# First loads on three queues, the position bias table behind the evictions, and four PSUM banks for the first projection of a two-block transformer kernel

## The chip, the cores and the metric

One core of one Trainium2 chip runs the kernel. The metric is the device time of one execution in microseconds; the time of before is the median of three runs. Engines are named as in the profile: PE is TensorE (PEld its weight loads), DVE VectorE, ACT ScalarE, POOL GpSimd, SP SyncE; a q behind the name means the engine's queue of DMA issues.

## What is computed

Two transformer blocks in a row on 512 tokens of width 1024, in float32. The change touches the start of the first block alone:

```
xn = rmsnorm(x, attn_norm_g)
proj = xn @ w_in                       # 1024 x 2312
qa, ka, va, qb, kb, vb, f_logit = split(proj)
qa, ka = rmsnorm per head of 64        # 8 query heads, 2 key heads
out_a = sliding-window attention (window 128) with sinks and the
        position bias  -slope_h * (t - s),  slope_h = 2 ** -(h + 1)
log_f = log_sigmoid(f_logit + b_forget);  c = cumsum(log_f over tokens)
out_b = causal softmax attention of qb, kb, vb with the bias c[t] - c[s]
x = x + concat(out_a, out_b) @ w_out
x = x + relu(rmsnorm(x) @ w_up) ** 2 @ w_down
```

The second block (conditioning, neighbourhood attention, pooling, a second MLP) follows and isn't touched.

## The kernel before

Every matrix operand is split into a high and a low float32r part (`split`, L147 and L148: ScalarE copies the high part, VectorE subtracts it), and a product is three matmuls, high by high, high by low, low by high (`mm3`, L152 to L154).

`attention_one` begins with the loads. The four token tiles `xin` (128 tokens by 1024) come by `fetch_x` (L346), the gain vector `g_attn` (128 x 8) by L349. The projection goes in six blocks c of output columns. Block 0 has 392 columns (four query heads, a key head, a value head, the 8 forget logits), and its weights come in four parts kp of 256 rows each; a part is fetched in four pieces of 256, 64, 64 and 8 columns (`part_of`, which calls `fetch`, L169). Then come the small loads of `misc`: four norm gains of 64 values (L365), the sinks, the forget bias and a few constants (L370 to L372), then `alibi0` (L376), a 128 x 256 table of distances, and the causal mask. All of these are issued by SyncE's queue, in the order of the code.

`project(0)` turns each token tile on TensorE (`turned`, L216, written `n_0t` to `n_3t` in the rows), splits it into `xnT`, multiplies the weight part by the gain and splits it (L183 on ScalarE gives `w_0h` to `w_3h`, L184 on VectorE `w_0l` to `w_3l`), and accumulates eight row groups for each token tile in one PSUM bank (`pj`). `close(t)` evicts a tile on ScalarE into `pjs`, scaled by the token's 1/rms (L407), and `finish` takes it to the head norm, the value tiles and the turned heads (`ta`, L490; `qa` and `kah` on ScalarE, L464 to L471). `square` (L256) makes the sum of squares of a token tile. Tiles 0 and 1 are accumulated side by side as the weight parts come; tiles 2 and 3 follow. The ring "x" of PSUM banks for `pj` has two banks, 0 and 1, so tile 2 needs the bank of tile 0, and its product can't begin before tile 0's eviction. When tile 2 is done, the loads of block 1 (`load(1)`) are asked for; block 1's rows read `w_0` to `w_3` too, with 384 columns. Two raw buffers hold its parts, so its third part is fetched when the first is split.

After `project_a(0)` ScalarE makes the position bias table of all heads, `alibi`, in eight activations from `alibi0` (L742), which the scores of the windowed attention read (L605). Then `gates` (L540 to L566) takes the forget logits `zf` through exp and log (`az`, L541 and L542), a cumulative sum on TensorE by a triangular matrix (`cps`, L558, from `trir` and `lfh`), and the attention of pairs of heads runs interleaved with the projection of the next block.

```
self.banks(x=(0, 1), o=(2,), t=(3, 4, 7), s=(5, 6))
...
for _ in project_a(0):
    pass
tab = self.gp.tile([P, 8, 256], F32, tag="g", name="alibi")
for h in range(8):
    ac(out=tab[:, h, :], in_=alibi0, func=AF.Copy, scale=-(2.0 ** -(h + 1)))
```

The code is written in this order, but each engine's own order of instructions is decided when the kernel is built, by a planner that follows a model of durations, and the loads' order on a queue with it. Each engine then works through its instructions in order.

Of the kernel before, what the change touches and what calls it, by code (L numbers as in the profile page):

```python
# [8 lines left out]
F32 = mybir.dt.float32  # L9
F32R = mybir.dt.float32r  # L10
AF = mybir.ActivationFunctionType
# [5 lines left out]
P = 128  # L17
SEQ = 512
D = 1024
# [12 lines left out]
C_ALIBI = 0  # L32
# [75 lines left out]
RB = 1.5  # L108
PBUF = 3
RATIO = 1.6  # L110
TURN = "vavp"
TURNA = "vvvp"
TURNB = "vvva"
# [16 lines left out]
class Build:  # L130
# [32 lines left out]

        return self.parts(name, self.fetch(name, srcs, a, b), a, b, gain, eng)

    def fetch(self, name, srcs, a, b, rv=None):
        rv = (self.raw(name) if rv is None else rv)[:, 0:a * b].rearrange("p (a b) -> p a b", a=a)
        for o, src in srcs:
            self.nc.sync.dma_start(out=rv[:, :, o:o + src.shape[2]], in_=src)  # L169
        return rv  # L170

    def parts(self, name, rv, a, b, gain=None, eng=None, own=None):
# [130 lines left out]
    def attention_one(self, ph):  # L303
        tc, nc, a = self.tc, self.nc, self.a
        tp = ph.enter_context(tc.tile_pool(name="t1", bufs=2, reuse_waits="tile"))
        cst = a["consts"]
        ac = nc.scalar.activation
# [3 lines left out]
        def const(name, shape, dt=F32):  # L311
            return tp.tile(shape, dt, name=name, tag=name, bufs=1)

        def prob(which, name, shape, dt=F32R):
            return tp.tile(shape, dt, tag="pt" + which, name=name, bufs=3)

        g = const("g_attn", [P, KC])
# [4 lines left out]
        for i in range(4):  # L322
            segs.append([(768 + 128 * i, 128), (1280 + 128 * i, 128), (1792 + 128 * i, 128)])

        def part_of(c, kp, rv=None):

            srcs, o = [], 0
            for s, w in segs[c]:
                srcs.append((o, self.kview(a["w_in"], 2 * kp, 2, s, w)))
                o += w  # L330
            return self.fetch(f"w{c}_{kp}", srcs, 2, o, rv), (2, o, g[:, 2 * kp:2 * kp + 2])

        def load(c):
            tiles = []
            for kp in range(4):
                rv, (n, w, gain) = part_of(c, kp)
                tiles.append(self.parts(f"w{c}_{kp}", rv, n, w, gain, nc.gpsimd if c > C1 and kp in KPG else None))
                yield 0.0
            loaded[c] = tiles
# [5 lines left out]
        def fetch_x(t):  # L345
            nc.sync.dma_start(out=xin[t], in_=a["x"][0, t * P:(t + 1) * P, :])  # L346

        fetch_x(0)
        nc.sync.dma_start(out=g, in_=a["attn_norm_g"].rearrange("(k p) -> p k", p=P))  # L349
        first = []  # L350
        for kp in range(4):
            first.append(part_of(0, kp, None if kp < 2 else prob("hl"[kp % 2], f"w0r{kp}", [P, D], F32)))
            if kp == 1:
                fetch_x(1)
        fetch_x(2)
# [2 lines left out]
        r1 = const("r1", [P, NT])  # L358
# [4 lines left out]
        for nm, col in gn.items():  # L363
            src = a[nm]
# [7 lines left out]
        nc.sync.dma_start(out=misc[:, 24:38], in_=cst[:, C_COEF:C_COEF + 14])  # L372
        for nm in ("q_norm_a", "q_norm_b"):
            nc.gpsimd.tensor_scalar(out=gn[nm], in0=gn[nm], scalar1=0.125, scalar2=0.0, op0=ALU.mult, op1=ALU.add)
        alibi0 = const("alibi0", [P, 256])
        nc.sync.dma_start(out=alibi0, in_=cst[:, C_ALIBI:C_ALIBI + 256])  # L376
        causal = const("causal", [P, P], F32R)
        identr = const("identr", [P, P], F32R)
        ctmp = tp.tile([P, P], F32, tag="p", name="ctmp", bufs=3)
# [5 lines left out]
        def project(c, finish):  # L385

            n = sum(w for _, w in segs[c])
            if c and c not in loaded:
                yield from load(c)
            tiles = loaded.pop(c) if c else []  # L390
            accs = {}

            def part(t, kp):
                if kp == 0:
                    accs[t] = self.ps("x", f"pj{c}_{t}")
                cols = slice(t * P, (t + 1) * P)
                wh, wl = tiles[kp]
                for i in range(2):
                    k = 2 * kp + i
                    xq = xnT[k // 4]  # L400
                    self.mm3(accs[t][:, 0:n], xq[:, k % 4, 0, cols], xq[:, k % 4, 1, cols], wh[:, i, :], wl[:, i, :],
                             k == 0, k == KC - 1)
                    yield 0.48

            def close(t):
                s = tp.tile([P, 392], F32, tag="pj", name=f"pjs{c}_{t}", bufs=2)
                ac(out=s[:, 0:n], in_=accs[t][:, 0:n], func=AF.Copy, scale=r1[:, t:t + 1])  # L407
                finish(t, s)

            def square(t):  # L410
                self.inv_rms(xin[t], r1, t, f"r1_{t}", self.part("wl", f"xs{t}", F32))

            turns = range(NT)
            if c == 0:
                turns = (2, 3)
                for kp in range(4):
                    if kp < 2:
                        self.split_T(xin[kp], xnT, kp, f"n1_{kp}")
                    rv, (a_, w, gain) = first[kp]
                    tiles.append(self.parts(f"w0_{kp}", rv, a_, w, gain))  # L420
                    if kp == 0:
                        yield from part(0, 0)
                    else:
                        if kp == 1:
                            yield from part(0, 1)
                            yield from part(1, 0)
                            yield from part(1, 1)
                        else:
                            square(kp - 2)
                            yield from part(0, kp)  # L430
                            yield from part(1, kp)
                for t in (2, 3):
                    self.split_T(xin[t], xnT, t, f"n1_{t}")
                for t in range(2):
                    close(t)
                    square(t + 2)
            for t in turns:
                for kp in range(4):
                    yield from part(t, kp)
                close(t)  # L440
                if t == NT - 2 and c + 1 < len(segs):
                    yield from load(c + 1)

        def head_norm(s, nh, name):

            w = 64 * nh
            sq = tp.tile([P, 384], F32, tag="sq", name=name + "sq", bufs=1)
            nc.gpsimd.tensor_tensor(out=sq[:, 0:w], in0=s[:, 0:w], in1=s[:, 0:w], op=ALU.mult)
            ss = self.small("ss", name + "ss")
            nc.vector.tensor_reduce(out=ss[:, 0:nh], in_=sq[:, 0:w].rearrange("p (h d) -> p h d", h=nh), axis=AX.X, op=ALU.add)  # L450
            r = self.rstd(ss[:, 0:nh], nh, 64, name + "r")
            qn = tp.tile([P, 384], F32, tag="qn", name=name + "qn", bufs=2)
            nc.gpsimd.tensor_tensor(out=qn[:, 0:w].rearrange("p (h d) -> p h d", d=64),
                                    in0=s[:, 0:w].rearrange("p (h d) -> p h d", d=64),
                                    in1=r[:, 0:nh].unsqueeze(2).to_broadcast([P, nh, 64]), op=ALU.mult)
            return qn
# [4 lines left out]
        def put_q(dst, src, gain, h, cols):  # L461

            me, other = slice(64 * h, 64 * h + 64), slice(64 - 64 * h, 128 - 64 * h)
            ac(out=dst[me, cols], in_=src[me, :], func=AF.Copy, scale=gain[me, :])  # L464
            stt(out=dst[other, cols], in0=src[me, :], scalar=gain[me, :], in1=dst[me, cols].bitcast(F32), op0=ALU.mult, op1=ALU.subtract)
# [34 lines left out]
        def project_a(i):  # L500
            pa = Pairs(f"ta{i}")

            def finish(t, s):
                if i == 0:
                    nc.vector.tensor_tensor(out=zf[:, t, :], in0=s[:, 384:392], in1=bfor, op=ALU.add)
                qn = head_norm(s, 5, f"a{i}{t}")
                self.split(va[i][0][:, t, 0:64], va[i][1][:, t, 0:64], s[:, 320:384])
                pa.put(t, [qn[:, 0:P], qn[:, P:2 * P], qn[:, 2 * P:2 * P + 64]])
                if t % 2 == 1:
                    cols = slice((t - 1) * P, (t + 1) * P)  # L510
                    for h in range(4):
                        put_q(qa[4 * i + h], pa.get(h // 2), gn["q_norm_a"], h % 2, cols)
                    put_k(*ka[i], pa.get(2), gn["k_norm_a"], 0, cols, True)
            yield from project(i, finish)
# [147 lines left out]
        def attn_b(pair, q, k, v):  # L662
# [61 lines left out]
            for x in range(len(units) + LA + 1):  # L724
# [8 lines left out]
                if y >= 0 and y % 2 == 1:  # L733
                    u, h, _ = units[y]
                    values(u, h)
                    yield CB * 0.8

        for _ in project_a(0):
            pass
        tab = self.gp.tile([P, 8, 256], F32, tag="g", name="alibi")  # L740
        for h in range(8):
            ac(out=tab[:, h, :], in_=alibi0, func=AF.Copy, scale=-(2.0 ** -(h + 1)))  # L742
        mixT.append(self.quad("mixT0"))
        b = {}
        gates()
# [258 lines left out]
    def attention_two(self, ph, hxT):  # L1004
# [90 lines left out]
        def attn(i, qT, kT, kcT, v, tb):  # L1095
# [3 lines left out]
            def scores(u, h, nn):  # L1099
# [16 lines left out]
                nc.vector.reciprocal(out=den[:, 0:1], in_=den[:, 0:1])  # L1116
                self.scaled(pr, den[:, 0:1], TURN[(2 * u + h) % 2 * 2 + nn])

# [105 lines left out]
        for i in range(4):  # L1224
            interleave(attn(i, *r[i]), fill[i], RATIO)

# [224 lines left out]
```

## Time and profile before

| what | us |
|---|---|
| median of 3 runs | 1255.92 (1253.18 to 1258.51) |
| the profiled execution's own time | 1260.07 |
| its span, first to last instruction | 1258.3 |
| TensorE busy | 1213.5 (96%) |
| VectorE busy | 844.6 (67%) |
| ScalarE busy | 567.3 (45%) |
| GpSimd busy | 355.1 (28%) |

The span is what the profile shows of the execution; 1.8 us of the time lie around it. Times in the rows count from the start of the span. A timeline row gives the start, the duration, the engine and line, the operation with output and inputs, how many instructions were merged (x8), and in brackets how long the engine was idle before and what released it. Names lose their numbers there: `w<-in_w_in_dram` is a piece of any weight part, `w_0h` the high part of kp 0 of any block; 392 columns are block 0, 384 a later one.

### The profile page before, as it was taken

The numbers are of one execution on the slowest core, as the hardware profiler recorded it, in microseconds if no ns is written. First come the engines' busy times: TensorE is split into PE (matmuls) and PEld (weight loads), VectorE is DVE, ScalarE is ACT, GpSimd is POOL, SyncE is SP. The second block draws the span as 40 slices with busy tenths as digits, with TensorE's granted clock in tenths as the row PEclk, the third lists the DMA queues.
The fourth block names the chain that finished last, engine by engine and source line by source line (L and its number), as shares of the span: only waits on it lengthen the run. The fifth ranks groups of instructions, "written<-read, shape, count | busy, mean of one in ns | idle before, by whom it ended". The sixth has DMA issues, their size and how long they took to land. (4 is left out here: it accounts for less than half of the span.)

```text
span 1258.3 us, 16992 instructions
## 1 busy us (share of the span) xinstructions
PE 1213.5 (96%) x6316; PEld 1017.5 (81%) x6316; DVE 844.6 (67%) x1410; ACT 567.3 (45%) x1068; POOL 355.1 (28%) x370
## 2 busy tenths in 40 slices
PE   7899999999999999999999999999899999999997
PEld 6898888779888878888889878777798888888885
DVE  3799766597898854346355557574868678777744
ACT  5576656434223313225254546463546454343431
POOL 2787552252010000000014124030642504205502
PEclk9899999999999999999999999999999999999999
DMA  6222222365678734134145311215443643524421
GB/s 165 64 60 53 57 63 68 101 183 154 197 220 258 240 119 138 67 101 135 67 151 157 84 53 52 85 38 201 124 162 102 185 123 117 147 81 134 150 68 67
DMA packets 151707, 150.71 MB, mean 120 GB/s; under 512 B 14345, under 2 KB 115480, under 8 KB 151624
## 3 DMA queue, kind: packets, MB, share of 16 engines
q1 hardware_dynamic: 147224, 139.41, 36.4%
q0 software_dynamic: 4400, 10.22, 2.6%
q8 instruction: 49, 0.80, 0.3%
q14 instruction: 34, 0.28, 0.1%
HBM read 143.24 MB, written 6.36 MB: 119 GB/s over the span
## 5 line engine op out<-in xcount | busy, mean ns | idle before, releaser
L1365 POOL TENSOR_TENSOR m2d<-m2d,m2d 128x1024 f32<-128x1024 f32 x24 | 71.2, 2981 | 162.2 <-DVE m2w220l L148 51.5
L898 DVE SCALAR_TENSOR_TENSOR macc<-mod,silu_c,macc 128x1024 f32<-128x1024 f32 x56 | 76.1, 1369 | 15.5 <-DMA mod<-in_w_mod_dram 15.2
L975 DVE SCALAR_TENSOR_TENSOR xa<-m1d,r,xa 128x512 f32<-128x512 f32 x32 | 23.8, 746 | 37.5 <-PE m1d L154 37.5
L918 POOL DMA_DIRECT2D modrows<-mrow x8 | 3.9, 492 | 146.4 <-DVE mrow L916 91.9
L147 ACT ACTIVATE m2hid<-m2sq 128x512 fp32r<-128x512 f32 (+1 forms) x32 | 17.6, 551 | 49.1 <-DVE m2sq L1328 49.1
L147 ACT ACTIVATE m1hid<-m1sq 128x512 fp32r<-128x512 f32 x32 | 20.0, 630 | 38.3 <-DVE m1sq L844 38.3
L148 DVE TENSOR_TENSOR npl<-t,nph 128x512 fp32r<-128x512 f32 x32 | 21.7, 682 | 16.4 <-ACT nph L147 16.3
L194 POOL TENSOR_SCALAR p<-p,d 128x512 f32<-128x512 f32 x8 | 14.0, 1752 | 57.1 <-DVE d L1116 27.3
L148 DVE TENSOR_TENSOR m2hid<-m2sq,m2hid 128x512 fp32r<-128x512 f32 (+1 forms) x32 | 24.3, 760 | 6.0 <-ACT m2hid L147 5.8
L181 POOL TENSOR_SCALAR w<-w,g_attn 128x384 f32<-128x384 f32 x20 | 25.8, 1297 | 9.1 <-DMA w<-in_w_in_dram 6.7
L148 DVE TENSOR_TENSOR m1hid<-m1sq,m1hid 128x512 fp32r<-128x512 f32 x32 | 22.0, 687 | 9.1 <-ACT m1hid L147 9.1
L683 DVE TENSOR_REDUCE mb<-sb 128x1 f32<-128x128 f32 (+3 forms) x32 | 15.6, 487 | 16.5 <-PE sb L680 16.4
L1115 ACT ACTIVATE p<-s,m 128x512 f32<-128x512 f32 x32 | 22.0, 688 | 5.8 <-DVE m L1113 5.8
L1069 POOL TENSOR_TENSOR tb<-G,nam 128x256 f32<-128x256 f32 x24 | 17.8, 774 | 22.1 <-DVE m L1109 12.5
L685 ACT ACTIVATE pb<-sb,mb 128x128 f32<-128x128 f32 (+3 forms) x32 | 16.8, 525 | 16.0 <-DVE mb L683 15.7
L843 ACT ACTIVATE m1re<-m1up 128x512 f32<-128x512 f32 x32 | 18.6, 583 | 10.1 <-PE m1up L154 9.8
L204 POOL TENSOR_SCALAR nc_0ss<-nc_0ss 128x1 f32<-128x1 f32 x1 | 0.2, 187 | 80.5 <-ACT nc_0x L256 80.5
L152 PE MATMUL pj<-w_0h,xnT 128*128 128x384 f32 (+1 forms) x48 | 18.0, 376 | 4.9 <-ACT pjs L407 3.9
L147 ACT ACTIVATE nph<-t 128x512 fp32r<-128x512 f32 x32 | 19.0, 595 | 7.5 <-PE t L1126 7.2
L981 POOL DMA_DIRECT2D xspill<-xa x4 | 2.6, 655 | 70.0 <-DVE xa L975 69.9
L844 DVE SCALAR_TENSOR_TENSOR m1sq<-m1up,m1re 128x512 f32<-128x512 f32 x32 | 21.8, 683 | 0.1
L1328 DVE SCALAR_TENSOR_TENSOR m2sq<-m2up,m2sq 128x512 f32<-128x512 f32 x32 | 21.9, 684 | 0.0
(2017 smaller groups left out, 4679.7 us busy)
## 6 DMA issues: line engine op xcount, KB each, us to landing
mod<-in_w_mod_dram SPq DMA_DIRECT2D x48, 512.0 KB, 4.6
m2d<-in_w_mlp_out_dram SPq DMA_DIRECT2D x44, 512.0 KB, 3.7
m1u<-in_w_up_dram SPq DMA_DIRECT2D x32, 512.0 KB, 4.3
m1d<-in_w_down_dram SPq DMA_DIRECT2D x32, 512.0 KB, 3.6
m2u<-in_w_mlp_in_dram SPq DMA_DIRECT2D x32, 512.0 KB, 4.1
w<-in_w_in_dram SPq DMA_DIRECT2D x16, 512.0 KB, 4.2
w<-in_w_in_dram SPq DMA_DIRECT2D x48, 128.0 KB, 2.6
o1w<-in_w_out_dram SPq DMA_DIRECT2D x8, 512.0 KB, 3.8
```

Source lines behind the costliest of these rows:

```text
L147: self.nc.scalar.activation(out=hi, in_=src, func=AF.Copy)
L148: (eng or self.nc.vector).tensor_tensor(out=lo, in0=src, in1=hi.bitcast(F32), op=ALU.subtract)
L152: mm(out=out, lhsT=lh, rhs=rh, start=start, stop=False)
L181: eng.tensor_scalar(out=rv[:, i], in0=rv[:, i], scalar1=g, scalar2=None, op0=ALU.mult)
L843: ac(out=r, in_=acc, func=AF.Relu)
L844: nc.vector.scalar_tensor_tensor(out=s, in0=acc, scalar=0.0, in1=r, op0=ALU.max, op1=ALU.mult)
L898: nc.vector.scalar_tensor_tensor(out=accs[s], in0=rw, scalar=sc[:, s, k:k + 1], in1=accs[s], op0=ALU.mult, op1=ALU.add)
L975: nc.vector.scalar_tensor_tensor(out=x[t][:, cols], in0=acc, scalar=r2[:, t:t + 1], in1=x[t][:, cols], op0=ALU.mult, op1=ALU.add)
L1069: nc.gpsimd.tensor_tensor(out=tb[:, h, y], in0=G[:, h, ::-1, o:o + 32][:, :, ::-1], in1=nam[:, y, :].unsqueeze(1).to_broadcast([P, 8, 32]) ...
L1115: ac(out=pr, in_=s, func=AF.Exp, bias=m[:, 2:3], accum_out=den[:, 0:1])
L1328: nc.vector.scalar_tensor_tensor(out=s, in0=acc, scalar=0.0, in1=s, op0=ALU.max, op1=ALU.mult)
L1365: pt(out=o, in0=x, in1=z, op=ALU.subtract)
```

## The change

`part_of` and `fetch` take a list of engines for the pieces. Part 0 of w_in is issued by ScalarE's queue; of part 1 the first piece stays on SyncE's, the other three go to GpSimd's. `g_attn` and `alibi0` are issued by GpSimd's queue, ahead of the weights. While `project_a(0)` is built, the ring "x" has the banks 5 and 6 as well, which the scores use later, so that each of its four token tiles has a bank of its own. And the eight activations of the table are ordered behind the last eviction of that projection (`issue_after(self.closed.ins)`).

```
+XMORE = (5, 6)
...
-    def fetch(self, name, srcs, a, b, rv=None):
+    def fetch(self, name, srcs, a, b, rv=None, engs=None):
         rv = (self.raw(name) if rv is None else rv)[:, 0:a * b].rearrange("p (a b) -> p a b", a=a)
-        for o, src in srcs:
-            self.nc.sync.dma_start(out=rv[:, :, o:o + src.shape[2]], in_=src)
+        for i, (o, src) in enumerate(srcs):
+            (engs[i] if engs else self.nc.sync).dma_start(out=rv[:, :, o:o + src.shape[2]], in_=src)
         return rv
...
         fetch_x(0)
-        nc.sync.dma_start(out=g, in_=a["attn_norm_g"].rearrange("(k p) -> p k", p=P))
+        alibi0 = const("alibi0", [P, 256])
+        nc.gpsimd.dma_start(out=g, in_=a["attn_norm_g"].rearrange("(k p) -> p k", p=P))
+        nc.gpsimd.dma_start(out=alibi0, in_=cst[:, C_ALIBI:C_ALIBI + 256])
         first = []
         for kp in range(4):
-            first.append(part_of(0, kp, None if kp < 2 else prob("hl"[kp % 2], f"w0r{kp}", [P, D], F32)))
+
+            engs = ([nc.scalar] * 4, [nc.sync, nc.gpsimd, nc.gpsimd, nc.gpsimd], None, None)[kp]
+            first.append(part_of(0, kp, None if kp < 2 else prob("hl"[kp % 2], f"w0r{kp}", [P, D], F32), engs))
...
-        alibi0 = const("alibi0", [P, 256])
-        nc.sync.dma_start(out=alibi0, in_=cst[:, C_ALIBI:C_ALIBI + 256])
...
-                ac(out=s[:, 0:n], in_=accs[t][:, 0:n], func=AF.Copy, scale=r1[:, t:t + 1])
+                self.closed = ac(out=s[:, 0:n], in_=accs[t][:, 0:n], func=AF.Copy, scale=r1[:, t:t + 1])
...
+        x_banks = self.rings["x"]
+        self.rings["x"] = x_banks + list(XMORE)
         for _ in project_a(0):
             pass
+        self.rings["x"] = x_banks
         tab = self.gp.tile([P, 8, 256], F32, tag="g", name="alibi")
-        for h in range(8):
-            ac(out=tab[:, h, :], in_=alibi0, func=AF.Copy, scale=-(2.0 ** -(h + 1)))
+        with tc.issue_after(self.closed.ins):
+            for h in range(8):
+                ac(out=tab[:, h, :], in_=alibi0, func=AF.Copy, scale=-(2.0 ** -(h + 1)))
```

The planner then orders the engines anew. Three places matter below. The first is ScalarE ahead of the first evictions. Before, where `w_0_397` is the raw tile of block 1's first part and `n_2t` the turned third token tile:

```order
L256 ACTIVATE xs_250,r_1ss<-xin_94 128x1024
L147 ACTIVATE xnT_122<-n_2t_267 128x4x128
L147 ACTIVATE xnT_123<-n_2t_274 128x4x128
L742 ACTIVATE alibi<-alibi_135 128x256 x8
L407 ACTIVATE pjs_0_295<-pj_0_175,r_124 128x392
L183 ACTIVATE w_0h<-w_0_397,g_attn 128x384 x2
```

Now:

```order
L257 ACTIVATE xs_250,r_1ss<-xin_94 128x1024
L184 ACTIVATE w_0h<-w_0_397,g_attn 128x384 x2
L148 ACTIVATE xnT_124<-n_2t_267 128x4x128
L410 ACTIVATE pjs_0_295<-pj_0_175,r_126 128x392
L148 ACTIVATE va0h<-pjs_0_295 128x64
L410 ACTIVATE pjs_1_319<-pj_1_208,r_126 128x392
```

The table is gone from here, and block 1's `w_0h` has come ahead of the third tile's `xnT` and of the first eviction.

The second place is ScalarE at the end of the projection, where `pjs_3` is the eviction of the fourth tile and `az` belongs to the gates. Before:

```order
L183 ACTIVATE w_2h<-w_2_417,g_attn 128x384 x2
L407 ACTIVATE pjs_3_462<-pj_3_437,r_124 128x392
L464 ACTIVATE qa<-ta_0_309,misc 64x256
L470 ACTIVATE kah_145<-ta_1_312,misc 64x256
L471 ACTIVATE kah_145<-ta_1_312,misc 64x256
L147 ACTIVATE va0h<-pjs_3_462 128x64
L541 ACTIVATE az<-az 128x32
L464 ACTIVATE qa<-ta_0_309,misc 64x256
L542 ACT_TABLE_LOAD
L542 ACTIVATE az<-az 128x32
```

Now:

```order
L184 ACTIVATE w_2h<-w_2_417,g_attn 128x384 x2
L410 ACTIVATE pjs_3_462<-pj_3_437,r_126 128x392
L749 ACTIVATE alibi<-alibi_98 128x256 x8
L148 ACTIVATE va0h<-pjs_3_462 128x64
L544 ACTIVATE az<-az 128x32
L467 ACTIVATE qa<-ta_0_309,misc 64x256
L473 ACTIVATE kah_145<-ta_1_312,misc 64x256
L474 ACTIVATE kah_145<-ta_1_312,misc 64x256
L545 ACT_TABLE_LOAD
L545 ACTIVATE az<-az 128x32
```

The eight activations of the table stand between the last eviction and the gates, and the second `qa` is behind the gates' second `az`.

The third place is VectorE around block 1's first low part (`w_0l` from the raw tile 397), with what each instruction waits for: DMAHW is a load, the others an engine. Before:

```order
L148 TENSOR_TENSOR xnT_123<-n_3t_288,xnT_123 128x4x128 [waits Activation_49]
L148 TENSOR_TENSOR va0l<-pjs_0_295,va0h 128x64 [waits Activation_49]
L148 TENSOR_TENSOR va0l<-pjs_1_319,va0h 128x64 [waits Activation_49]
L450 TENSOR_REDUCE a01ss<-a01sq 128x5 [waits Pool_49]
L184 SCALAR_TENSOR_TENSOR w_0l<-w_0_397,g_attn,w_0h 128x384 [waits DMAHW6_49,DMAHW0_49,DMAHW7_49,DVE_49,PE_49]
L184 SCALAR_TENSOR_TENSOR w_0l<-w_0_397,g_attn,w_0h 128x384
```

Now:

```order
L149 TENSOR_TENSOR xnT_124<-n_3t_281,xnT_124 128x4x128 [waits Activation_49]
L149 TENSOR_TENSOR xnT_125<-n_3t_288,xnT_125 128x4x128 [waits Activation_49]
L453 TENSOR_REDUCE a01ss<-a01sq 128x5 [waits Pool_49]
L185 SCALAR_TENSOR_TENSOR w_0l<-w_0_397,g_attn,w_0h 128x384 [waits DMAHW2_49,DMAHW3_49,DMAHW1_49,Activation_49]
L185 SCALAR_TENSOR_TENSOR w_0l<-w_0_397,g_attn,w_0h 128x384
L508 TENSOR_TENSOR zf<-pjs_2_378,misc 128x8 [waits Activation_49]
```

The place is nearly the same, but `w_0l` waits for loads and ScalarE alone, no longer for PE.

On the queues the order is this. SyncE: token tile 0, the first piece of part 1, token tile 1, parts 2 and 3, token tiles 2 and 3, the small loads, the causal mask, then block 1. ScalarE: the four pieces of part 0, ahead of its first table load. GpSimd: `g_attn` and `alibi0` ahead of finishing the identity matrix `ident`, then three pieces of part 1. On TensorE all transposes of tiles 0 and 1 now come ahead of the first product, and the second half of tile 3's transposes comes behind the first product of tile 2.

## Rows read from the trace of the kernel before

**Rows 1.** The page, part 1, the line of busy time.
```profile
PE 1213.5 (96%) x6316; PEld 1017.5 (81%) x6316; DVE 844.6 (67%) x1410; ACT 567.3 (45%) x1068; POOL 355.1 (28%) x370
```

**Rows 2.** Stretches: busy us (instructions) of PE, PEld, DVE, ACT, POOL; granted clock, DMA share, GB/s.
```profile
0.00:36.00 36.00, 26.72 (x129) 24.70 (x130) 14.28 (x28) 20.34 (x42) 12.84 (x27) 0.95 0.54 146
...
10.00:15.00 5.00, 4.80 (x23) 4.03 (x21) 2.18 (x4) 3.26 (x7) 0.74 (x2) 1.00 1.02 288
...
25.60:35.90 10.30, 10.27 (x48) 10.24 (x49) 5.29 (x12) 6.38 (x14) 9.66 (x13) 0.83 0.12 37
47.30:53.40 6.10, 6.10 (x16) 4.79 (x17) 4.31 (x13) 4.46 (x10) 4.52 (x4) 0.50 0.38 88
60.00:80.00 20.00, 19.45 (x129) 18.57 (x129) 19.13 (x66) 16.56 (x49) 18.45 (x20) 1.00 0.33 80
```

**Rows 3.** Timeline of TensorE: start, us, instruction, [idle before, releaser].
```profile
21.87 0.71 PE L216 MATMUL n_3t<-ident,xin 128*128 128x128 f32 x5
25.63 0.45 PE L152 MATMUL pj<-w_0h,xnT 128*128 128x392 f32 x1 [3.06 <-ACT pjs L407]
...
35.73 0.34 PE L154 MATMUL pj<-w_3h,xnT 128*128 128x392 f32 x1
...
47.26 0.77 PE L558 MATMUL cps<-trir,lfh 128*128 128x512 f32 x1 [2.85 <-DVE trir L554]
```

**Rows 4.** Timeline of ScalarE, first 45 us.
```profile
0.72 1.28 ACT L147 ACT_TABLE_LOAD   x1 [0.72 <-PEq L1444]
5.78 0.60 ACT L147 ACTIVATE xnT<-n_0t 128x512 fp32r<-128x512 f32 x1 [3.78 <-PE n_0t L216]
...
22.55 2.56 ACT L742 ACTIVATE alibi<-alibi 128x256 f32<-128x256 f32 x8 [3.07 <-DMA alibi<-in_consts_dram]
25.01 0.57 ACT L407 ACTIVATE pjs<-pj,r 128x392 f32<-128x392 f32 x1
25.48 1.11 ACT L183 ACTIVATE w_0h<-w,g_attn 128x384 fp32r<-128x384 f32 x2
...
38.05 1.12 ACT L183 ACTIVATE w_2h<-w,g_attn 128x384 fp32r<-128x384 f32 x2 [3.53 <-DMA w<-in_w_in_dram]
39.08 0.57 ACT L407 ACTIVATE pjs<-pj,r 128x392 f32<-128x392 f32 x1
40.77 0.47 ACT L464 ACTIVATE qa<-ta,misc 64x256 fp32r<-64x256 f32 x1 [1.13 <-PE ta L490]
...
44.29 0.23 ACT L542 ACTIVATE az<-az 128x32 f32<-128x32 f32 x1
```

**Rows 5.** Timeline of SyncE's queue, first 60 us (issues alone).
```profile
1.63 4.17 SPq L169 DMA_DIRECT2D w<-in_w_in_dram  x8
...
18.66 0.43 SPq L376 DMA_DIRECT2D alibi<-in_consts_dram  x1
...
19.69 3.24 SPq L169 DMA_DIRECT2D w<-in_w_in_dram  x6
...
34.38 18.47 SPq L169 DMA_DIRECT2D w<-in_w_in_dram  x15
```

**Rows 6.** Transfers from 15 to 25 us, GB/s in 40 slices of 0.25 us.
```profile
GB/s 229 148 33 33 33 0 1 1 0 0 0 0 0 0 1 1 2 3 3 2 5 3 4 2 2 7 217 340 373 385 371 315 288 345 329 334 295 246 228 104
```

**Rows 7.** Timeline of GpSimd near 239 us.
```profile
239.15 0.92 POOL L877 DMA_DIRECT2D silu_c<-in_c_dram  x1
```

**Rows 8.** DMA issues of the first 60 us: count, KB each, median us to landing.
```profile
w<-in_w_in_dram SPq DMA_DIRECT2D x12, 64.0 KB, 3.3
...
g_attn<-in_attn_norm_g_dram SPq DMA_DIRECT2D x1, 4.0 KB, 3.9
```

**Rows 9.** DMA issues of the whole span, by GpSimd.
```profile
g_mod<-modrows POOLq DMA_DIRECT2D x4, 4.0 KB, 3.1
...
silu_c<-in_c_dram POOLq DMA_DIRECT2D x1, 4.0 KB, 6.2
```

**Rows 10.** Who waited for whom, first 60 us: us in total, times, longest.
```profile
DVE w_0l L184 <- PE pj L153: 2.2, 1, 2.2
```

More of the change, by code (lines that the diff above doesn't have):

```diff
@@ L323, in attention_one, with part_of @@
             segs.append([(768 + 128 * i, 128), (1280 + 128 * i, 128), (1792 + 128 * i, 128)])
-        def part_of(c, kp, rv=None):
+        def part_of(c, kp, rv=None, engs=None):
             srcs, o = [], 0
@@ L330, in part_of @@
                 o += w
-            return self.fetch(f"w{c}_{kp}", srcs, 2, o, rv), (2, o, g[:, 2 * kp:2 * kp + 2])
+            return self.fetch(f"w{c}_{kp}", srcs, 2, o, rv, engs), (2, o, g[:, 2 * kp:2 * kp + 2])
         def load(c):
```

## The prediction

> **What bounds the kernel now.** I began with the page: TensorE is busy for 1213.5 us, 96% of the span [rows 1], so a change off its path is worth nothing, and only its waits can give time back. The table by stretches says where to look [rows 2]: of the first 36 us it is busy for 26.72, so 9.3 us are idle there. That is the first projection, the stage that the change touches.
>
> The timelines name the waits. On TensorE the product for the third token tile starts at 25.63 us after 3.06 us of idle time, released by an eviction (`pjs`, L407), and the first product of the gates (`cps`) at 47.26 us after 2.85 us, released by the triangular matrix [rows 3]. On ScalarE eight table activations start at 22.55 us, after 3.07 us of waiting for their load, and only then, at 25.01 us, comes the eviction that frees the bank [rows 4]. So the first wait is made of the load of `alibi0`, 2.46 us of table, and the eviction.
>
> That load is late because of what stands ahead of it in one queue: SyncE needs 4.17 us for eight pieces of w_in and issues `alibi0` at 18.66 us [rows 5]. But the transfers are not short of issues: between 10 and 15 us the 16 engines show a busy share of 1.02 at 288 GB/s [rows 2]. From 16.25 to 21.25 us next to nothing moves, 0 to 5 GB/s in slices of 0.25 us, while the small loads of `misc` go through, and the big loads behind them start near 21.5 us [rows 6].
>
> Both waits cost clock as well. Behind the first the granted clock of 25.6 to 35.9 us is 0.83, which is 1.8 us of 10.3 lost; behind the second that of 47.3 to 53.4 us is 0.50, the lower level of 1.2 GHz, which is 3 us lost [rows 2].
>
> **The change, part by part.** *Three queues.* w_in part 0 goes to ScalarE's queue; g_attn, alibi0 and three pieces of part 1 to GpSimd's. ScalarE gains four issues ahead of its table load; at 0.52 us each (4.17 us for eight [rows 5]) they end near 2.8 us and the table load of 1.28 us near 4.1 us, before its first work at 5.78 us [rows 4]: no cost. GpSimd issues two loads ahead of finishing `ident`. The nearest row, a load of the same 128 x 8 pattern, took 0.92 us to issue [rows 7], so `ident` comes near 3 us, ahead of that first work on transposes: no cost. g_attn took 3.9 us to land by SyncE's queue [rows 8]; such vectors took 3.1 to 6.2 us by GpSimd's [rows 9], so it is there at 4 to 7 us. The new order asks for it only behind the transposes of both first tiles, which covers even 7 us.
>
> What the three queues bring is the question. By the rows, bytes and not issues fill the time to 15 us; the bytes up to the fourth token tile stay the same, with 0.13 MB of alibi0 among them. I take their end as unmoved, 16 us, by the nearest row, the share of 1.02. Ends: 2 us earlier if several queues at once reach the 340 to 385 GB/s that the same engines move near 22 us [rows 6]; 1 us later if they get in each other's way. The Trainium skill, "DMA: Bandwidth & Descriptors", section "Issuing engines are not separate DMA queues", says that loads started by different engines run on the same 16 DMA engines and interleave, and that only the issue time is saved, "which is usually small relative to the DMA itself"; by that rule the bulk ends no earlier and the sum is the one below, where the faster row alone would give the first rival's 1249.6. The share of 1.02 agrees with it.
>
> *Four banks and the table.* The third tile's product no longer needs the eviction, and the eight activations leave that place. But ScalarE works in order, and in the new order the next block's `w_0h` stands ahead of the third tile's `xnT`; its load is the next big thing behind the small loads. Its third piece is issued at 19.69 plus two steps of 0.54 (3.24 us for six [rows 5]), 20.77, and lands 3.3 us later [rows 8]: 24.1 us. The queue has lost one issue, alibi0's, 0.43 us [rows 5], so 23.7 us. Then `w_0h` takes some 1.0 us to the next start and `xnT` 0.6 us [rows 4]: TensorE starts the third tile at 25.3 instead of 25.63. **Gain 0.3 us of the 3.06**, and four transposes of the fourth tile now come behind the wait instead of ahead of it: at 0.71 us for five [rows 3] 0.57 us. Net 0.3 us later at the end of the projection. The wait stays, with a load for a releaser, and I take the lower clock behind it to stay.
>
> *Behind the projection.* Here the table costs and the order gives. In the old order VectorE's `w_0l` of the next block waits 2.2 us for a product [rows 10], and only at 34.38 us SyncE issues the next part [rows 5]; ScalarE sits 3.53 us for it, scales it at 38.05 us and evicts the fourth tile (`pjs`) at 39.08 us [rows 4], 3 us after the last product ends (35.73 and 0.34 [rows 3]). In the new order `w_0l` waits for no product. It then comes some 2.2 us earlier, and so do the load, the scaling and that eviction: 36.9 us. Now the eight activations follow. From the eviction's start the new chain has 0.5 us for it, 2.46 us for the table, and of the old 3.52 us from the first `qa` to the logarithm of the gates (40.77 to 44.29) all but the second `qa` of 0.47 us, 3.05 us [rows 4]: 6.0 us, so the logarithm comes at 42.9 instead of 44.29. The first gate product follows it by 2.97 us as before (44.29 to 47.26 [rows 3, 4]): 45.9 instead of 47.26. **Gain 1.4 us.** The 0.3 us of the projection lie inside, as the eviction chain and not TensorE sets this place.
>
> **Sum.** 1.4 us, seen at the gates. The order behind it also moves, but the same work is done. The profiled execution took 1260.07 us, 4.2 us over the median of the three runs; 1.4 us off gives 1258.7 against its own time and 1254.5 us against the median of 1255.92.
>
> **Rivals.** *The loads do come earlier.* If the bulk ends 2 us sooner, the small loads and the next block's weights shift with it, the third tile starts with hardly a wait, and 3.06 us and the 1.8 us of lower clock go: 4.9 us, with the 1.4 us 6.3 us, 1249.6. For it: three queues fill the first 2 us, in which one queue has only begun [rows 5]. Against it: the share of 1.02 [rows 2], and that the five quiet microseconds stay whole in SyncE's queue [rows 6]. 22 in 100.
>
> *The block at `w_0h` gets worse: slower than before.* If the queues hinder each other and that load lands 1.1 us later than it did, at 25.2 us, ScalarE can't make `xnT` and TensorE starts the third tile at 26.8: 1.1 us lost. Then the part `w_2` comes no earlier, and of the table's 2.46 us ahead of the gates only ScalarE's idle 1.13 us [rows 4] is cover: 1.3 us more, and up to 1.1 us if the lower clock lasts longer. Together 2.4 to 3.5 us, up to 1259.4. It decides once the load lands behind 24.1 us. For it: all four tiles' evictions stand in order behind one load. Against it: one issue less is ahead of that load. 15 in 100.
>
> *Nothing is kept.* Between 60 and 80 us VectorE is busy for 19.13 of 20 us [rows 2]; a start 1.4 us earlier, with another order of the attention's units, may be lost there: 1256. For it: VectorE, GpSimd and TensorE all stand above nine tenths there. Against it: the whole stage starts earlier, with all its engines. 20 in 100.
>
> **How the numbers follow.** The forecast has 43 in 100, the three rivals 22, 15 and 20. About half a per cent, 6.3 us, is what a measurement of this kernel can tell from no change. Faster than that: half of the first rival, which lies just on that line, and a small part of the forecast in which the 3 us of clock behind the gates go and the attention's order helps: 0.20. Slower than that needs more than the second rival's price: 0.06. The rest, 0.74, is within. The range goes from 1247.5 (the first rival with 2 us of the gates' clock) to 1259.5 (the second).
>
> **What would show it.** Right: the first gate product 1 to 2 us earlier; the third tile's first product near 25 us, with ScalarE's `w_0h` waiting for a load ahead of it; next to no transfers for about 5 us behind the fourth token tile; the eight activations between the last `pjs` and `az`. Wrong: a third tile before 24 us (first rival), one after 26 us (second), or gates early and the attention's end not (third). If the bulk ends before 15 us, the step on the queues has failed.

## The result and the profile after

The changed kernel took 1264.76 us, the median of 13 executions (1258.18 to 1270.12), beside 1256.88 us for the kernel before: a ratio of 1.0065 (95% interval 1.005 to 1.008). It is slower, by about 8 us, where 1254.5 us was forecast and 1259.5 us was the upper end. The profiled execution of after is one of its quicker ones (1262.53 us, span 1260.8 us).

The front came as the prediction had it. The page's busy line of after, which answers to [rows 1]:

```profile
PE 1213.2 (96%) x6316; PEld 1014.5 (80%) x6316; DVE 845.4 (67%) x1410; ACT 567.4 (45%) x1068; POOL 355.5 (28%) x375
```

The stretches of [rows 2], with the same columns:

```profile
0.00:36.00 36.00, 26.04 (x136) 24.50 (x137) 13.24 (x29) 18.20 (x35) 16.65 (x34) 1.00 0.57 155
10.00:15.00 5.00, 3.92 (x13) 3.35 (x13) 3.78 (x7) 4.34 (x9) 0.00 (x0) 1.00 0.82 210
25.60:35.90 10.30, 10.02 (x59) 9.87 (x59) 5.28 (x15) 6.16 (x15) 9.19 (x15) 1.00 0.18 40
47.30:53.40 6.10, 5.93 (x19) 5.10 (x20) 3.94 (x7) 4.27 (x10) 4.07 (x4) 0.54 0.22 53
60.00:80.00 20.00, 18.34 (x120) 17.14 (x118) 18.07 (x64) 14.17 (x43) 17.25 (x18) 1.00 0.24 57
```

The timelines of TensorE and of ScalarE, which answer to [rows 3, 4]:

```profile
25.27 0.45 PE L153 MATMUL pj<-w_0h,xnT 128*128 128x392 f32 x1 [1.65 <-ACT xnT L148]
...
46.11 0.77 PE L561 MATMUL cps<-trir,lfh 128*128 128x512 f32 x1 [1.34 <-DVE trir L557]
```

```profile
23.62 1.12 ACT L184 ACTIVATE w_0h<-w,g_attn 128x384 fp32r<-128x384 f32 x2 [5.44 <-DMA w<-in_w_in_dram]
24.65 0.57 ACT L148 ACTIVATE xnT<-n_2t 128x512 fp32r<-128x512 f32 x1
25.12 0.58 ACT L410 ACTIVATE pjs<-pj,r 128x392 f32<-128x392 f32 x1
...
36.75 0.57 ACT L410 ACTIVATE pjs<-pj,r 128x392 f32<-128x392 f32 x1
37.22 2.55 ACT L749 ACTIVATE alibi<-alibi 128x256 f32<-128x256 f32 x8
...
42.55 0.23 ACT L545 ACTIVATE az<-az 128x32 f32<-128x32 f32 x1
```

The third token tile starts at 25.27 us (forecast 25.3), `pjs_3` at 36.75 (36.9), the logarithm at 42.55 (42.9), the first gate product at 46.11 (45.9), 1.15 us ahead of before. ScalarE waits 5.44 us for the next block's load, since the transfers of 15 to 25 us (GB/s in 40 slices, as [rows 6]) still have their five quiet microseconds:

```profile
GB/s 393 459 393 311 99 18 1 1 0 0 0 0 0 1 1 1 3 3 3 4 3 2 3 4 11 116 324 379 379 307 299 363 344 335 275 282 214 206 385 416
```

So the loss lies behind the gates. From the start of the first gate product to the end of the last value product (`ob`) of the last causal pair, the first attention lasted 191.9 us before (47.26 to 239.15) and 195.3 us after (46.11 to 241.40). The rows that end it, before and after:

```profile
238.81 0.34 PE L577 MATMUL ob<-pbh,vb3l 128*64 128x128 f32 x2
...
241.06 0.34 PE L580 MATMUL ob<-pbh,vb3l 128*64 128x128 f32 x2
```

Aligned row by row, by names without their numbers, the two traces differ between 47 and 700 us in some 850 TensorE, 350 VectorE and 220 ScalarE rows, though the change names none of them. Most lie in the attention; 94 of TensorE's lie in the dense block behind it (output projection and first MLP).

### The profile page after: what moved, and what is told of

The parts are those of the page before. It is cut to its first block, busy times and chain, and to the rows that moved or that the text cites. A ratio compares the mean times of both kernels' runs of the same rounds, so it can differ in the third digit from the quotient of the medians.

```text
span 1260.8 us, 17011 instructions
## 1 busy us (share of the span) xinstructions
PE 1213.2 (96%) x6316; PEld 1014.5 (80%) x6316; DVE 845.4 (67%) x1410; ACT 567.4 (45%) x1068; POOL 355.5 (28%) x375
```

## Experiments

**The order against the front.** What the planner chose anew can be taken apart from what the change says. A table `ORDER` holds, engine by engine, the places in which the planner of the other kernel put the instructions of a stage, and each instruction is ordered behind the one ahead of it (issue order only, no wait):

```
+        n0 = len(nc.cur_bb.bb.instructions)
         gates()
...
+        for i in nc.cur_bb.bb.instructions[n0:]:
+            if "Boundary" not in type(i).__name__:
+                own.setdefault(str(i.engine).split(".")[-1], []).append(i)
+        for eng, places in ORDER.items():
+            row = [own[eng][k] for k in places]
+            for p, q in zip(row, row[1:]):
+                tc.add_manual_dep(q, p.name, mybir.DependencyInfo(mybir.DependencyClass.NoSync, mybir.DependencyReason.DATA), reason="order")
```

In x1 the changed kernel gets the order of before from the gates to the end of that attention; in x2 the kernel before gets that of after. What the code lists ahead of the gates stays the planner's: some `qa` and `kal` of the first projection, which run among the attention's rows, stand elsewhere in x1 than before.

> The changed kernel (loads on three queues, table late, four banks), but from the gates to the end of the first attention every engine keeps the order of instructions that it had before the change, on TensorE all 1156 instructions of that stage. Theory A, the order that the planner chose anew for attention costs the time: the front is 1 to 1.2 us ahead at the first gate product and the old order keeps that, so a ratio to before of 0.998 to 1.000 (1254 to 1257 us), the gates' first product near 46.1 us and the last product of that attention 1 to 2 us earlier than before. Theory B, the loads on three queues or the four banks cost it by themselves: the ratio stays at 1.005 to 1.008 (1263 to 1267 us). Theory C, the time goes to stretches of the lower clock that any change of the front brings: the ratio is near 1.005 at a lower mean granted clock, with the pieces between such stretches as long as before.

> The kernel before with its own front (one queue, table ahead of the evictions, two banks), but from the gates to the end of the first attention every engine has the order of the changed kernel. Theory A (the order costs the time): slower than before by 1.005 to 1.008, 1263 to 1267 us, with the loss between 50 and 245 us. Theory B (the loads or banks): 0.999 to 1.001. Theory C (clock alone, by any change): about 1.005 with a lower granted clock.

x1: 1.0017 (1.0002 to 1.0032). x2: 1.0072 (1.0044 to 1.0101). The order alone, on a front that nobody touched, costs as much as the whole change, and the change with the old order is nearly the kernel before. Theory A holds and B falls; C has a part, since four of x2's six executions have a mean clock of 0.985 or 0.986 and took 1268.8 us or more, while the other two, at 0.993 and 0.989, took 1262.3 us, still 5.8 us above before. Theory A's figure for x1 missed: the gates came at 46.37 us, but nothing was kept. VectorE shows where the lead went. Its timeline near 63 us and GpSimd's, first in x1, then in the kernel before:

```profile
63.10 2.72 DVE L190 SCALAR_TENSOR_TENSOR w_2l<-w,g_attn,w_2h 128x384 fp32r<-128x384 f32 x2 [0.15 <-ACT w_2h L189]
...
62.56 0.94 POOL L200 TENSOR_SCALAR p<-p,da 128x256 f32<-128x256 f32 x1
63.46 1.95 POOL L154 TENSOR_TENSOR w_1l<-w,w_1h 128x768 fp32r<-128x768 f32 x1
```

```profile
63.76 1.15 DVE L184 SCALAR_TENSOR_TENSOR w_2l<-w,g_attn,w_2h 128x384 fp32r<-128x384 f32 x2
...
64.36 2.24 POOL L148 TENSOR_TENSOR w_1l<-w,w_1h 128x768 fp32r<-128x768 f32 x1
```

Until 56 us VectorE ran 1.88 us ahead of before; by 63 us, after some waits for ScalarE, 0.66 us of that was left. Then two `w_2l`, which take 1.15 us together, took 2.72 us (0.62 and 2.19): GpSimd's `w_1l` had started 0.36 us behind the first of them, and the second ends at 65.82 us, 0.41 us behind the end of `w_1l` at 65.41. In before the same two start 0.60 us ahead of `w_1l`, and it is `w_1l` that takes longer. The Trainium skill, "SBUF — State Buffer", section "SBUF: two separate sides", says that VectorE (with two SBUF inputs, for one) and GpSimd hold a port pair "for the whole instruction; the other fully blocks"; the rows agree for `w_1l`, which reads two tensors. For `p`, which reads one, they agree only where the starts are close: in after `p` took 1.34 us instead of 0.93 beside a `w_2l` that began 0.08 us ahead of it, and in y4 a `w_2l` that began 0.04 us behind `p` took 0.85 us instead of 0.62; but in x1 the first `w_2l` began 0.54 us into `p` (62.56 to 63.50 us) and took its usual 0.62. VectorE is busy in x1 for 37.07 of the 40 us from 60 to 100, and what it lost wasn't made up: on TensorE a row that came 1.6 us ahead of before at 58.5 us comes 0.15 us behind it at 66.3 us.

**Each part alone.** x3 has the queues alone, x4 the table's place alone, with the planner's own order; x5 to x8 have parts of the change with the order of before from the gates on.

```
x3, x5: engs, g_attn and alibi0 as in the change; one ring "x", table where it was
x6:     self.rings["x"] = x_banks + list(XMORE) alone
x4, x7: with tc.issue_after(self.closed.ins): alone
x8:     x6 and x7 together
```

> Only the first loads on three engines' queues; table and banks as before; the planner orders the rest anew (about 1300 of 6140 TensorE rows stand elsewhere). Theory A (order): whatever the new order gives, anywhere from 0.996 to 1.008, and the first gate product within 1 us of before's 47.3 us, since the queues bring the front nothing. Theory B (loads): 1.005 or more, with the loss ahead of the gates, at 47 us.

> Only the eight activations of the table ordered behind the last eviction of the first projection; one queue and two banks as before. The eviction that frees the bank then has no table ahead of it: the third token tile starts some 2.5 us earlier than 25.63 us, near 23 us, and the table's 2.5 us lie between the last eviction and the gates, so the first gate product comes at 46 to 48.5 us. Theory A: the total then hangs on the order chosen for attention, 0.996 to 1.008. Theory B (loads or banks cost the time): no loss here, 0.998 to 1.001.

> The queues alone, and from the gates to the end of the first attention the order of instructions of the kernel before. With the order chosen anew the queues alone gave 1.0063. Theory A (the order is what costs): back to 0.997 to 1.001; the first gate product near 45.9 us as with the queues alone, 1.4 us ahead of before, and the table made near 9 us. Theory B (the loads cost it): 1.005 or more.

> The four banks alone, with the order of before from the gates on. The table stays ahead of the first eviction, but the third token tile has its own bank: its first product follows the transposes of the fourth tile without the 3.06 us of waiting, near 22.3 us instead of 25.63. The eviction of the fourth tile still waits for the next block's second load, so the gates move by less than 1 us. Theory A: 0.997 to 1.001. Theory B with the banks (the scores' banks held up by late evictions): 1.003 or more.

> The table's order alone, with the order of before from the gates on. With the order chosen anew it gave 1.0111, with a third tile that started at 22.03 us (3.6 us earlier) and a first gate product at 49.06 us (1.8 us later, since the table lies between the last eviction and the gates). Theory A: the 1.8 us at the gates stay and the rest of the 14 us goes: 1.000 to 1.003. Theory B (the table's place itself costs it): 1.008 or more.

> Banks and table without the queues, with the order of before from the gates on. If parts add and the order is the cost, this is x6 and x7 together, 0.999 to 1.003, and what it lacks against the whole change with the old order (1.0017) is what the queues do: below 1.0017 they cost time, above it they save some.

| part | planner's order | order of before |
|---|---|---|
| queues | x3 1.0063 (1.0039 to 1.0087) | x5 1.0027 (1.0005 to 1.0048) |
| table | x4 1.0111 (1.0085 to 1.0137) | x7 1.0023 (0.9999 to 1.0047) |
| banks | | x6 1.0005 (0.9986 to 1.0025) |
| banks and table | | x8 1.0044 (1.0026 to 1.0062) |

With the old order more than half of each loss goes, and no part gains. x5 and x8 lie above what their expectations allowed: the fronts do cost a little, and hardly in sum, as banks and table cost more without the queues (x8) than with them (x1, 1.0017), though the two intervals touch. In x8 the first gate product comes only at 50.59 us, 3.3 us later than before; why the queues cure that wasn't followed up. The table's place alone removes the wait that the change is aimed at, and the gates are later for it. TensorE and ScalarE of x4, beside [rows 3, 4]:

```profile
22.03 0.42 PE L152 MATMUL pj<-w_0h,xnT 128*128 128x392 f32 x1
...
49.06 0.77 PE L558 MATMUL cps<-trir,lfh 128*128 128x512 f32 x1 [1.53 <-DVE trir L554]
```

```profile
38.64 0.59 ACT L407 ACTIVATE pjs<-pj,r 128x392 f32<-128x392 f32 x1 [1.75 <-POOL a01qn L453]
39.12 2.25 ACT L743 ACTIVATE alibi<-alibi 128x256 f32<-128x256 f32 x7
```

The third tile starts 3.6 us earlier than at 25.63, but the last eviction only 0.44 us earlier than at 39.08, and now the table stands between it and the gates, 1.8 us later than before. All six executions of x4 have a low mean clock too (0.983 to 0.985), so its 1.0111 isn't the price of waits alone. In x3 the planner made the table at 8.74 us, as `alibi0` had landed, and the gates came at 45.86 us without any new place for it.

**Which engine, which part of the stage.** x9 repeats the change. x10 keeps the old order only behind about 100 us, in the causal pairs; x11 keeps it on TensorE alone. x12 is the kernel before with `RA = (1.2, 1.45)` for `(1.2, 1.5)`, which moves 788 TensorE rows behind 75 us.

> The changed kernel once more, beside the runs below. Theory A (the order of attention): 1.005 to 1.008 as first measured; its attention, from the first gate product to the last product of the last pair, takes 195 to 197 us against 191.9 before and 194.1 with the old order. Theory C (the lower clock makes up the rest): its runs spread by 8 us or more, the slower ones at a lower mean granted clock, and a profile of a slower one shows more stretches at half clock than that of a quick one with the same waits.

> The changed kernel; the old order is kept only in the later part of the first attention (the causal pairs, traced behind the windowed ones), while the windowed part, which runs to about 100 us, is ordered by the planner anew. If the cost sits in the windowed part: 1.005 to 1.008 as the whole change. If it sits in the causal pairs: 1.001 to 1.003, as with the old order throughout (1.0017).

> The changed kernel with the old order on TensorE's queue alone; VectorE, ScalarE and GpSimd are ordered anew around it (some 100 VectorE and 50 ScalarE instructions stand elsewhere than in x1). If the order on TensorE is what costs: 1.001 to 1.003, as x1. If VectorE's and ScalarE's order costs: 1.004 to 1.008.

> The kernel before with one planner number changed: the weight with which the second windowed pair is mixed with the next projection goes from 1.5 to 1.45. Up to about 75 us nothing moves; behind that 788 TensorE rows stand elsewhere. No load, bank or table is touched. Theory A in its strong form (the order of before is a good one among many, and nearly any other costs): 1.003 to 1.008. In its weak form (only the order that the change brings is bad): 0.998 to 1.002.

x9: 1.0057 (1.0038 to 1.0077). x10: 1.0008 (0.999 to 1.0027). x11: 1.0061 (1.0039 to 1.0083). x12: 1.0035 (1.0015 to 1.0054). The loss comes with the order of the causal pairs, not with that of the windowed part, where x9 and x10 run alike to 0.3 us. One thing moves along in x10: with the old order in the pairs the planner also arranged the dense block as before (no row of TensorE, VectorE or ScalarE differs between 243 and 700 us, against 94 of TensorE's in after). The attention's order suffices without it: in x2 no row of TensorE's dense block differs from before either. x11 doesn't say which engine's order costs, since TensorE's old order among the others' new one made TensorE wait, as the list of its waits from 46 to 120 us shows (in total, times, longest):

```profile
PE pj L158 <- ACT pjs L415: 8.1, 3, 5.2
PE sa L609 <- ACT p L618: 3.7, 2, 2.9
```

And x12 suggests that the order of before is a good one: one nudge to one number of the planner cost 0.35%.

What costs in the causal pairs: first the waits of TensorE from 100 to 300 us in x9, then in x10.

```profile
PE n_1t L217 <- DVE xg L947: 3.0, 1, 3.0
PE o L153 <- DVE mixT L149: 1.9, 1, 1.9
PE tb L706 <- DVE pb L195: 0.9, 1, 0.9
PE ob L580 <- ACT pbh L148: 0.7, 1, 0.7
PE ob L580 <- DVE pbl L149: 0.4, 1, 0.4
```

```profile
PE n_2t L222 <- DVE xg L966: 2.7, 1, 2.7
PE o L158 <- DVE mixT L154: 1.9, 1, 1.9
PE tb L711 <- DVE db L694: 0.9, 1, 0.9
PE o L158 <- ACT mixT L153: 0.2, 1, 0.2
```

The last value products wait 0.7 and 0.4 us for their weights; of the 2.6 us by which x9 ends the attention later (243.03 against 240.40), that is 1.1. Some 30 us ahead of them stand the last product of the last projection and the first score of the last pair, here in x9 and then in x10:

```profile
208.51 0.34 PE L155 MATMUL pj<-w_3h,xnT 128*128 128x384 f32 x1
...
211.81 0.49 PE L153 MATMUL sb<-kb3h,qb3h 64*128 64x128 f32 x2
```

```profile
202.22 0.34 PE L160 MATMUL pj<-w_3h,xnT 128*128 128x384 f32 x1
...
214.60 0.32 PE L158 MATMUL sb<-kb3h,qb3h 64*128 64x128 f32 x1
```

The new order projects the last pair 6 us later and scores it at once, so that its first score is even 2.8 us earlier. In before that product starts at 200.97 us, in after at 206.91. That the late projection makes the value products wait isn't shown, and y1 and y5 below speak against it.

**Which pairs.** y1 keeps the old order in the last pair alone, y2 in the dense block behind the attention alone, y5 in both; y3 is x10's mirror, the kernel before with the new order in the causal pairs; y6 is x10 again; y4 has queues and banks without the table's new place, with the old order in the causal pairs.

> The changed kernel; the old order is kept for the last pair of causal heads alone (from about 215 us to the end of that attention). In the profile of the whole change the last products of that pair wait 0.69 and 0.40 us for the weights' high and low part, which the old order doesn't show. If the loss sits in the end of the attention: 1.001 to 1.003, and these two waits are gone. If it is spread over the pairs or sits in the dense block: 1.004 to 1.007.

> The changed kernel with its own order throughout attention; the old order is kept in the dense block behind it (output projection and first MLP, about 243 to 690 us) alone, which moves 176 TensorE and 84 VectorE rows. Of the 6.7 us between the profiles of the whole change and of the old order behind 100 us, 2.9 us stand at the end of attention, 1.7 us come between 260 and 300 us and 2.1 us later. If the dense block's order costs: up to 3.8 us come back, 1.002 to 1.004. If it is the attention's order that costs there too (through what it leaves late): 1.005 to 1.007.

> The kernel before, all of its front and its windowed attention, with the changed kernel's order in the causal pairs alone: the mirror of x10. If that order is the cause: 1.004 to 1.008, with the gates at the time of before and the loss behind 100 us. If it costs only together with the new front: 0.999 to 1.002.

> Queues and four banks without the table's new place (the planner then makes the table near 9 us, off every later path), with the old order in the causal pairs: what the experiments so far point to as the best form of the change. The first gate product should come near 45 to 46 us. If VectorE's full stretch from 50 to 100 us swallows the front's gain, as in x1: 0.999 to 1.002, no better than before. If the gain is kept: 0.997 to 0.999.

> The changed kernel with the old order in the last causal pair and in the dense block behind it, nowhere else: 194 TensorE and 96 VectorE rows differ from the changed kernel. If these two places are the whole cause: 1.000 to 1.002, as x10. If the first three pairs' order costs as well: 1.003 to 1.005. In the profile the waits of 0.69 and 0.40 us at the last value products are gone.

> The same kernel as x10, on this chip and beside y5: 1.000 to 1.003 if x10's 1.0008 holds.

y1 1.0052 (1.003 to 1.0074), y2 1.0056 (1.0035 to 1.0076), y5 1.0043 (1.0022 to 1.0065), y6 1.0014 (0.9999 to 1.0029), y3 1.0048 (1.003 to 1.0066). The new order of the causal pairs, with the dense block that the planner arranges behind it (94 TensorE rows, as in after), is enough to slow the kernel before down (y3). Each single place brings little back, and by the median both together (y5) leave most of the loss. In y1, y3 and y5 the last projection still comes late (208.97, 208.35 and 208.07 us): it is mixed with the third pair, whose order y1 and y5 leave new. The waits of 0.7 and 0.4 us are gone in the profiles of y1 and y5 all the same, so they belong to the last pair's own order.

Part of the loss comes with the clock. Stretches of y5, then of y6 (columns as [rows 2]):

```profile
100.00:228.00 128.00, 127.67 (x800) 110.63 (x799) 90.65 (x254) 76.34 (x207) 59.89 (x74) 0.99 0.20 55
228.00:245.20 17.20, 16.71 (x58) 12.26 (x59) 8.10 (x21) 7.29 (x20) 0.65 (x1) 0.50 0.09 30
```

```profile
100.00:228.00 128.00, 128.00 (x809) 111.11 (x808) 93.37 (x259) 79.02 (x215) 62.21 (x75) 1.00 0.20 55
228.00:245.20 17.20, 14.23 (x81) 11.27 (x80) 9.44 (x22) 6.61 (x16) 5.30 (x7) 0.90 0.39 136
```

From 228 to 245 us y5 ran at 0.50, the lower level of 1.2 GHz, and did 58 matmuls where y6 did 81; its attention ended at 247.46 us, y6's at 238.98. Ahead of it TensorE was busy for 127.67 of 128 us at 0.99, with one wait of 0.19 us; what makes the clock fall there isn't shown.

y5's twelve executions fall into two groups. Four have a mean clock of 0.993 to 0.995 and a mean span of 1254.9 us, no longer than y6's; eight, the profiled one among them, have 0.990 or less and a mean span of 1263.0 us, and none lies between 1256.2 and 1260.7 us. The gap of 8 us is about what the stretch at 0.50 cost the profiled one at the end of the attention (8.5 us), and 17.1 us at half clock lower the mean clock by 17.1 x 0.5 / 1261 = 0.007, as far apart as the groups are. So with the old order in these two places what is left of the loss comes with the clock; that all eight have the same stretch is inferred, from one profile.

The same sorting can be tried on the others, with care: the groups are small, they come from different chips, and in the kernel before, too, clock and time go together (74 of its 135 executions beside the experiments have 0.991 or more, at a mean span of 1253.5 us, 17 have 0.988 or less, at 1258.7). After and x9 have 7 of 25 at 0.988 or less, at 1267.1 us; x10 and y6 none of 24. The profiles of after and x9 have no such stretch from 228 to 245 us, so where their clock falls in those seven isn't shown. At 0.991 or more the mean spans are 1261.0 us for after and x9, 1259.9 for y1, 1257.9 for y2, 1254.9 for y5 and 1256.1 for x10 and y6. By this some 5 us of the loss are there without the lower clock, and they go with the last pair (about 1 us, as its waits of 1.1 us) and the dense block (about 3 us). How the dense block's order costs them was not followed up.

y4, what seemed the best form, had the earliest gates (44.92 us), but an attention of 198.6 us, 6.7 us longer than before: 1.0027 (1.0012 to 1.0041). No version beat the kernel before.

## Why the prediction was wrong

- *Three queues cost nothing and bring nothing; the bulk ends at 16 us.* Right: the slices fall from 311 to 18 GB/s between 15.75 and 16.5 us. That the bulk ended no earlier agrees with the Trainium skill's rule on issuing engines ("DMA: Bandwidth & Descriptors", "Issuing engines are not separate DMA queues"). The premise that the engines stay full didn't hold: the share from 10 to 15 us went down to 0.82, at 210 GB/s, and from 15 to 16 us the slices show up to 459 GB/s.
- *The third tile gains 0.3 us and waits for a load.* Right: 25.27 us, behind ScalarE's `xnT`, behind `w_0h` and its 5.44 us of waiting for the load. *The lower clock behind it stays:* wrong in this execution (1.00 instead of 0.83), so the projection's last product came at 35.33 us, 0.4 us earlier than before instead of 0.3 later. As forecast, the eviction chain and not TensorE set the gates.
- *The gates gain 1.4 us.* Right to 0.25 us: 1.15 us.
- *"The order behind it also moves, but the same work is done."* This step failed. It counted at nothing an order that x2 measures by itself at 1.0072, some 9 us, and y3, its causal pairs with the dense block behind them, at 1.0048. The same work is done, but with other waits and, in part of the executions, at a lower clock. The front with the old order is 1.0017 (x1); the rest of 1.0065 is the order, as far as the two add.
- *The sum is the gain at the gates.* Wrong as well, and by itself too small to matter: with the old order x1 had its gates 0.9 us earlier and its time didn't fall.
- *The third rival, nothing is kept,* had the front right: with the old order the 1 us gained is lost by 66 us, in VectorE's full stretch. But it had no price beyond the gain, and looked at 60 to 80 us, where the loss is behind 100 us; there TensorE of before is busy for 128.00 of the 128 us from 100 to 228, so that no wait pointed at it. The second rival's mechanism, the load at `w_0h`, didn't occur.
- The range was built from the waits of the front. The prediction quoted three pieces of the changed order around them and priced only those.

## What to carry to other kernels

Where a planner orders a kernel as a whole, a change of ten instructions is a change of all: count the moved rows behind the edit, and if there are hundreds in a tuned stage, put the price of an order into the range; here kernels with another order than before's (x2, x3, x4, x12) stood 0.35 to 1.1% above it. To find out whether an edit or the new order moved the time, give the new kernel the old order and the old kernel the new one. Look, too, at how the executions of one kernel are spread: y5's median hid two groups 8 us apart, and each says something else. And a wait removed ahead of a stage that another engine fills may be worth nothing: x4's third tile came 3.6 us earlier and x1's gates 0.9 us, and neither total fell.

## What the runs showed that was not expected

One nudge of one planner number (x12) cost 4.4 us by itself. VectorE's two `w_2l` took 1.15 us where GpSimd's `w_1l` started 0.60 us behind the first, and 2.72 us where it started 0.36 us behind it, so a start 0.66 us earlier ended 0.9 us later. The lower clock lasted 17 us at a place with hardly a wait (y5: 127.67 of the 128 us before it busy).
